# The low halves of the plain weights made by a scaling on ScalarE and an adding transfer from DRAM, with some modulation work and the feed-forward products in another order

## The chip, the cores and the metric

The kernel runs on one core of a Trainium2 chip. The time is the device time of one execution in microseconds (us), from the first instruction to the last, with what the runtime puts around it. The engines are called as in the profile: PE (TensorE, matrix products; PEld is its weight load), DVE (VectorE), ACT (ScalarE), POOL (GpSimd) and SP (SyncE, which issues most transfers). Every engine works through its own queue of instructions strictly in order.

## The reference

One inference step of one hybrid layer: an HGRN2 mixer (a gated linear recurrence, 8 heads) and a Hyena mixer (a short convolution and a long one) stand beside each other, followed by a SwiGLU feed-forward. There are 128 prompt tokens and 512 sample tokens, 640 in all, the model width is 1024, the feed-forward width 2816. Cut to what matters here:

```
mod = silu(cond) @ ada_w + ada_b          # shift, scale, gate, twice
h = x * (1 + scale1) + shift1
proj = h @ w_in                           # 1024 -> 10240 columns
q, f_fwd, f_bwd, i_raw, g_raw, hy, mg = split(proj)
o_a = hgrn2_mixer(q, f_fwd, f_bwd, i_raw, g_raw, ...)
o_b = hyena_mixer(hy, ...)
gate_a, gate_b = split(sigmoid(mg))
mix = (gate_a * (o_a @ proj_a) + gate_b * (o_b @ proj_b)) @ w_out
x = layer_norm(ALPHA * x + gate1 * mix)
h = x * (1 + scale2) + shift2
gt, up = split(h @ ffn_w_in)              # 1024 -> 2 x 2816
x = layer_norm(ALPHA * x + gate2 * ((silu(gt) * up) @ ffn_w_out))
```

Everything is float32.

## The kernel before

**Split precision.** PE multiplies in a rounded 32-bit type (fp32r in the profile). To keep float32 precision each weight and each operand is split into a high half, its rounded copy, and a low half, what the rounding left. Each product is then three passes: high by high, operand's low by high, high by weight's low. So a tile of weights needs one cast (`wh`, the high half) and one subtraction (`wl` = raw - `wh`) before its third matmul can run.

**Two kinds of weight tiles.** *Plain* weights go through one stream of 101 tiles of 128x1024 (512 KB each), in the order in which the products use them: `issue` (L346) allocates a `raw` tile (3 buffers), starts its load on SP, casts it to `wh` (on ACT at L357 for most, on DVE for some, by the string `HIE`) and subtracts to get `wl` (L181, the line of the helper for two-operand operations; on DVE, for a few early ones on POOL by `WSUB`). `wh` and `wl` have 3 buffers (slots) each, so a tile's cast waits until the unit of products three tiles earlier has let go of its slot. `advance` (L361) decides how many tiles ahead are issued. The second kind are weights of two stages that use a Strassen-like scheme with 7 products instead of 8 (class `Wino`, L626 on): `gate` loads and splits the first raw tile of a block j (`wfg` in the feed-forward), `rest` loads the second and forms sums and differences of both in place (`rf`), with splits of each (`wfa`, `wfs`, `wfu`, `wfv`). These use the same `raw` buffers.

**The stages**, by the profile's time: start, filters and tables (to about 120 us); most of `w_in` by the seven-product scheme (m1, 115 to 330); the convolution by Fourier products, 330 to 516; `proj_b` (516 to 579); the recurrence, head by head, with its own plain products (579 to 878); `proj_a` (878 to 934); `w_out` (934 to 1003); the first feed-forward product by the seven-product scheme, 22 blocks (1004 to 1282); the second, called `fo`, 22 plain units of 30 matmuls of 128x512 (1282 to 1433); the last layer norm (to 1442).

**What sets the order.** In m1 the string `PLAN` is the order: `gJ` and `wJ` are gate and rest of block J, `NJ` is product N of block J, `Qi` is half a product of the modulation with `ada_w` (`ada_quad`, L400), after which the load of the next half of `ada_w` is issued (`ada_next`, L863: `araw`, 1 MB, on POOL's queue at L397). Every second `Q` is followed by `ada_vec` (L414), which copies the product out of PSUM on ACT (`md`, L417) and transposes it on PE (`adaT`, L430) or sums it there (`adag`, L420). In the feed-forward the tuple `PERIOD` is the order inside a period j: gate and rest of the next block, then the products. Product 7 of a block is copied out by ACT (`fu`, L676) before product 4 of that block may add to the same bank (`fa`). A scheduler then places every instruction in its engine's queue, within these orders and by what it takes the durations to be.

Of the kernel before, what the change touches and what calls it, by code (L numbers as in the profile page):

```python
# [13 lines left out]
ALU = mybir.AluOpType  # L14
# [101 lines left out]
    return {k: np.ascontiguousarray(v) for k, v in c.items()}  # L116


PLAN = """x0 k0 L0 k1 x4 k2 p mlp t L1 T0 x3 T4 A0 x2 D0 T2 A1 x1 L2 B0 M0 T1 D2 A2 M2 T3 h0 L3 B1 D1 A3 h1 B2 M1 D3 h2 h3 M3 h4 W2 W0 h5 h6 h7 W1 q V0 e0 B3 g0 W3 V1 m w0 e2 10 20 g1 50 11 60 g2 70 21 30 40 w1 w2 61 51 52 12 71 Q8 62 22 g3 w3 13 41 g4 53 72 Q9 42 31 63 w4 g5 23 14 w5 73 Q10 43 32 g6 w6 64 24 15 54 74 Q11 33 65 25 44 16 26 55 75 Q12 g7 34 w7 66 45 56 17 76 Q13 35 67 46 g8 27 57 w8 18 77 Q14 g9 g10 36 w9 28 19 68 37 29 58 78 Q15 69 47 59 w10 79 Q16 38 110 210 g11 610 49 111 510 39 48 w11 211 g12 611 112 w12 212 710 Q17 g13 511 711 Q18 410 113 w13 311 612 310 411 512 712 Q19 513 213 613 412 713 312 413 313"""
HMOD = "SVSSVSSS"  # L120
HSUB = "GVVVVGVG"
WSUB = "VGGVVGGG"
# [6 lines left out]
FFNP = "1-1 2-1 g1 w1"  # L129
FFNT = ("g2", "", "")  # L130
FFN0 = "51 61 12 22 w2 71"
PERIOD = (("g", 1), ("w", 1), ("6", 0), ("4", -1), ("1", 1), ("5", 0), ("7", 0), ("3", -1), ("2", 1))
WPRI = 2
HIE = """SSSSVVSVSVSSSSSSSVVVSVVSVSSVSSSSSSSSSSSSSSSSSSSSSSSSSSSSSSSSSSSSSSSSSSSSSSSSSSSSSSSSSSSSSSSSSSSSSSSSSSSSSSSSSS"""
LOOK = """22222012202102201120122111222222222222222222222222222222222222222222222222222222222222222222222222222222222222"""
# [27 lines left out]
def body(tc, I, O):  # L163
    nc = tc.nc
    V, S, G, PE, SY = nc.vector, nc.scalar, nc.gpsimd, nc.tensor, nc.sync
# [14 lines left out]
    def tt(out, a, b, op, eng=None):  # L180
        return (eng or V).tensor_tensor(out=out, in0=a, in1=b, op=op)  # L181
# [4 lines left out]
    def f32(ap):  # L186
        return ap.bitcast(F32)

    def pool(name, bufs=1, space=None, side=None):
        kw = dict(name=name, bufs=bufs, reuse_waits="tile")  # L190
        if space is not None:
            kw["space"] = space
        if side is not None:
            kw["side"] = side
        cm = tc.tile_pool(**kw)
        p = cm.__enter__()
        return p, (lambda: cm.__exit__(None, None, None))
# [19 lines left out]
    def mm_bank(nm):  # L217
        return bank("mm", nm)
# [20 lines left out]
    w1 = sp.tile([EMB, ORD], F32, name="w1")  # L239
# [12 lines left out]
    w2 = sp.tile([P, ORD], F32, name="w2")  # L252
    w3 = sp.tile([P, 2, ORD], F32, name="w3")
# [92 lines left out]
    def issue(i):  # L346
        src, (a, b), own = stream["specs"][i]
        raw = wp.tile([P, a, b], F32, tag="raw", bufs=RAW_BUFS, name=f"raw{i}")
        SY.dma_start(raw, src)
        if own is None:  # L350
            q, th, tl, n = wp, "wh", "wl", HL_BUFS
        else:
            q, th, tl, n = own[0]["p"], "wbh", "wbl", own[1]
        hi = q.tile([P, a, b], F32R, tag=th, bufs=n, name=f"wh{i}")
        lo = q.tile([P, a, b], F32R, tag=tl, bufs=n, name=f"wl{i}")
        with tc.high_priority():
            (V.tensor_copy if HIE[i] == "V" else S.copy)(hi, raw)  # L357
            tt(lo, raw, f32(hi), ALU.subtract, G if i < len(WSUB) and WSUB[i] == "G" else V)
        stream["hl"].append((hi, lo))

    def advance(pos, n):  # L361
# [33 lines left out]
    def ada_load(nb, i, q, tag, bufs, eng=SY):  # L395
        raw = q.tile([P, 4, 512], F32, tag=tag, bufs=bufs, name=f"araw{nb}_{i}")
        eng.dma_start(raw, ada_w.rearrange("(k p) n -> p k n", p=P)[:, 4 * i:4 * i + 4, nb * 512:nb * 512 + 512])  # L397
        ada["raw"][nb, i] = raw
# [9 lines left out]
    def ada_mods(nb, q):  # L408
        with tc.high_priority():
            for i in range(2):  # L410
                ada_quad(nb, i)
            ada_vec(nb, q)

    def ada_vec(nb, q):  # L414
        part, half = nb // 2, nb % 2
        md = q.tile([P, 512], F32, tag="md", bufs=1, name=f"md{nb}")
        S.copy(md, ada["ps"].pop(nb))  # L417
        if part in (2, 5):
            p2 = mm_bank(f"adag{nb}")
            PE.matmul(p2[0:2, :], cst[:, 128:130], md, start=True, stop=True)  # L420
            gr = q.tile([2, 512], F32, tag="md", bufs=1, name=f"gr{nb}")
            SY.dma_start(gr, I["ada_b"][:, nb * 512:nb * 512 + 512].to_broadcast([2, 512]))
            tt(gr, p2[0:2, :], gr, ALU.add)
            V.tensor_scalar(gr, gr, 1.0 / ALPHA, None, ALU.mult)
            SY.dma_start(gd[part // 3, :, half * 512:half * 512 + 512], gr)
            return
        slot = {0: 0, 1: 1, 3: 2, 4: 3}[part]
        p2 = mm_bank(f"adaT{nb}")
        for i in range(4):
            PE.transpose(p2[:, i * P:i * P + P], md[:, i * P:i * P + P], ident)  # L430
        v = p2.rearrange("p (k g r) -> p k g r", k=4, g=4)[:, :, :, 0:2]
        dst = modT[:, slot, half * 4:half * 4 + 4, :]
        b0 = 17 + slot * 8 + half * 4
        tt(dst, v[:, :, 0], prT2[:, b0:b0 + 4].unsqueeze(2).to_broadcast([P, 4, 2]), ALU.add)
        for g in range(1, 4):
            tt(dst, v[:, :, g], dst, ALU.add)
# [3 lines left out]
    vp, close_vp = pool("vp")  # L440
# [7 lines left out]
    def x_load(t):  # L448
        xs = se.tile([P, D], F32, tag="xs", bufs=3, name=f"xs{t}")
        SY.dma_start(xs, x_tok[t])  # L450
        return xs

    def x_transpose(t, xs):
        for q in range(2):
            ps = sc_bank(f"xT{t}_{q}")
            for k in range(4):
                PE.transpose(ps[:, k * P:k * P + P], xs[:, (4 * q + k) * P:(4 * q + k + 1) * P], ident)
            for i in range(2):
                cpy("x", 2 * t + q, xT.tiles[2 * q + i][:, :, t * P:t * P + P],
                    ps[:, i * 256:i * 256 + 256].rearrange("p (k t) -> p k t", k=2))  # L460
# [162 lines left out]
    class Wino:  # L623
# [98 lines left out]
    def start():  # L722
        stream["stop"] = 4
        xs, ld, ab = {}, {}, {}

        def step(op, i):
            if op == "x":
                xs[i] = x_load(i)
            elif op == "T":
                x_transpose(i, xs[i])  # L730
            elif op == "L":
                ld[i] = kern_load(i)
            elif op == "A":
                ab[i] = kern_a(i, ld[i])
            elif op == "B":
                ab[i] = kern_b(i, ab[i])
            elif op == "W":
                kern_store(i, ab[i])
            elif op == "k":
                ktab(i)  # L740
            elif op == "D":
                for n in range(2):
                    ada_load(i, n, se, "araw", 3)
            elif op == "Q":
                nb, n = divmod(i, 2)
                ada_quad(nb, n)
                if i < M1_ADA[1] * 2 - 1:
                    ada_next(i + 1)
                if n == 1:
                    ada_vec(nb, mo["y"])  # L750
            elif op == "M":
                ada_mods(i, se)
            elif op == "h":
                make_h(i)
            elif op == "V":
                run_unit(vu[i])
            elif op == "e":
                m1_operands(i)
            elif op == "m":
                m1_open()  # L760
            elif op in "gw1234567":
                m1.run(op + str(i))()
            else:
                dict(p=params_load, t=params_T, q=params)[op]()

        for tok in PLAN.split():
            if tok == "mlp":
                if HP:
                    with tc.high_priority():
# [12 lines left out]
    mo = {}  # L782
# [78 lines left out]
    m1 = Wino("m", lambda tag: mo["p"], m1_x, m1_cols, m1_done, M1PRI)  # L861

    def ada_next(i):  # L863
        ada_load(*divmod(i, 2), vp, "v", 1, G)

    def m1_open():
        close_sp()
# [917 lines left out]
```

## Time and profile before

| what | number |
|---|---|
| time, median of 3 runs | 1445.78 us (1444.48 to 1446.87) |
| the profiled execution | 1444.85 us; its span is 1442.4 us |
| PE busy | 1382.4 us, 96% of the span |
| DVE, ACT, POOL busy | 998.9, 617.4, 72.6 us |
| mean granted PE clock | 0.992 of full speed |
| moved by DMA | 195.63 MB, 136 GB/s over the span |

Times in a row are microseconds from the start of the span. A row of a timeline reads: start, length, engine, line, operation, output<-inputs, shapes, count, and in brackets how long the engine had been idle and what ended that. A row of a table of groups reads: line, engine, operation, names, shapes, count, then busy us and mean ns of one, then the engine's idle time ahead of them and who ended it. A row of the DMA issues ends with the median us from issue to landing. A row of the waits says which engine and tile waited for which: us in total, times, longest.

### The profile page before, as it was taken

What the parts mean: (1) busy time and instruction counts of PE and PEld (TensorE: products, weight loads), DVE (VectorE), ACT (ScalarE), POOL (GpSimd) and SP (SyncE); (2) the same over time, 40 slices, a digit from 0 to 9 for tenths busy, and PEclk for the clock granted to TensorE, in tenths of its full rate; (3) what the DMA queues carried; (4) which work ended last, traced back from release to release, by engine and by line L of the source; (5) the groups of instructions that cost most, each with busy time, mean ns of one, the idle gap of its engine ahead of it and who ended that gap; (6) DMA issues with size and microseconds to landing.
All of it is one profiled execution on the core that took longest, in us unless ns stands there. A gap on an engine that the chain in (4) does not pass through costs nothing. (4 is left out here: it accounts for less than half of the span.)

```text
span 1442.4 us, 23457 instructions
## 1 busy us (share of the span) xinstructions
PE 1382.4 (96%) x9513; PEld 1297.4 (90%) x9513; DVE 998.9 (69%) x1751; ACT 617.4 (43%) x1011; POOL 72.6 (5%) x68
## 2 busy tenths in 40 slices
PE   5999999989999999999999999999999999999997
PEld 2698888889999998999999999988999999998886
DVE  6886775745888853638888786568977667756427
ACT  3654544432333211446665655227644344542111
POOL 4320000011000000000000000000000000000003
PEclk9999999999999999999999999999999999999999
DMA  7934665557333364432232223551343333257211
GB/s 245 327 136 139 210 194 156 169 183 251 96 92 92 107 211 146 144 119 83 63 102 61 76 57 113 180 182 73 109 123 104 108 115 106 88 177 278 83 59 73
DMA packets 195783, 195.63 MB, mean 136 GB/s; under 512 B 7581, under 2 KB 155773, under 8 KB 194908
## 3 DMA queue, kind: packets, MB, share of 16 engines
q1 hardware_dynamic: 188524, 167.17, 37.1%
q0 software_dynamic: 5424, 21.73, 4.3%
q10 hardware_dynamic: 1728, 5.24, 0.9%
q8 instruction: 74, 1.21, 0.3%
q14 instruction: 33, 0.27, 0.1%
HBM read 162.91 MB, written 31.21 MB: 135 GB/s over the span
## 5 line engine op out<-in xcount | busy, mean ns | idle before, releaser
L181 DVE TENSOR_TENSOR wl<-raw,wh 128x1024 fp32r<-128x1024 f32 x96 | 117.3, 1224 | 133.4 <-ACT wh L357 132.4
L357 ACT CAST wh<-raw 128x1024 fp32r<-128x1024 f32 x90 | 94.1, 1049 | 221.2 <-PE pb L611 41.0
L1423 PE MATMUL fo<-wh,act 128*128 128x512 f32 (+1 forms) x440 | 130.7, 380 | 0.0
L1423 PEld LDWEIGHTS fo<-wh,act 128*128 128x128 f32 x440 | 81.3, 188 | 15.9
L1423 PE MATMUL fo<-wl,act 128*128 128x512 f32 (+1 forms) x220 | 83.4, 379 | 0.0
L611 PE MATMUL hy<-hTh,wh 128*128 128x320 f32 x256 | 79.6, 311 | 0.0
L611 PE MATMUL hy<-hTh,wl 128*128 128x320 f32 x256 | 79.2, 309 | 0.0
L611 PE MATMUL hy<-hTl,wh 128*128 128x320 f32 x256 | 79.2, 309 | 0.0
L611 PE MATMUL f<-hTh,wh 128*128 128x320 f32 x224 | 70.8, 316 | 0.0
L611 PE MATMUL f<-hTl,wh 128*128 128x320 f32 x224 | 69.7, 311 | 0.0
L611 PE MATMUL f<-hTh,wl 128*128 128x320 f32 x224 | 69.3, 309 | 0.0
L181 POOL TENSOR_TENSOR y<-y,gb 128x512 f32<-128x512 f32 x8 | 11.6, 1454 | 900.8 <-ACT y L170 900.5
L1423 PEld LDWEIGHTS fo<-wl,act 128*128 128x128 f32 x220 | 41.4, 188 | 7.9
L611 PEld LDWEIGHTS hy<-hTh,wh 128*128 128x128 f32 x256 | 48.1, 188 | 0.0
L611 PEld LDWEIGHTS hy<-hTl,wh 128*128 128x128 f32 x256 | 48.1, 188 | 0.0
L611 PEld LDWEIGHTS hy<-hTh,wl 128*128 128x128 f32 x256 | 48.1, 188 | 0.0
L170 ACT ACT_TABLE_LOAD x36 | 46.2, 1283 | 1.4 <-PEq L1769 0.7
L707 PE MATMUL v<-wl,hTh 128*128 128x256 f32 x160 | 44.9, 285 | 1.6 <-DVE wl L181 1.6
L707 PE MATMUL v<-wh,hTl 128*128 128x256 f32 x160 | 45.1, 285 | 0.2 <-POOL hTl L181 0.2
L707 PE MATMUL v<-wh,hTh 128*128 128x256 f32 x160 | 44.8, 285 | 0.0
L611 PEld LDWEIGHTS f<-hTl,wh 128*128 128x128 f32 x224 | 42.2, 188 | 0.0
L611 PEld LDWEIGHTS f<-hTh,wh 128*128 128x128 f32 x224 | 42.2, 188 | 0.0
(2291 smaller groups left out, 4730.9 us busy)
## 6 DMA issues: line engine op xcount, KB each, us to landing
raw<-in_w_in SPq DMA_DIRECT2D x52, 512.0 KB, 3.8
rf<-in_ffn_w_in SPq DMA_DIRECT2D x42, 512.0 KB, 4.0
araw<-in_ada_w POOLq DMA_DIRECT2D x16, 1024.0 KB, 5.7
rm<-in_w_in SPq DMA_DIRECT2D x28, 512.0 KB, 3.8
raw<-in_ffn_w_out SPq DMA_DIRECT2D x22, 512.0 KB, 3.7
sd<-my SPq DMA_DIRECT2D x28, 320.0 KB, 3.6
araw<-in_ada_w SPq DMA_DIRECT2D x8, 1024.0 KB, 11.3
kk<-kd SPq DMA_DIRECT2D x20, 256.0 KB, 3.1
```

Of the source, the lines that this page charges most:

```text
L170: r = S.activation(out, in_, func, bias=bias, scale=scale)
L181: return (eng or V).tensor_tensor(out=out, in0=a, in1=b, op=op)
L357: (V.tensor_copy if HIE[i] == "V" else S.copy)(hi, raw)
L611: r = PE.matmul(ps[:, 0:HT], w[a][:, k, :], x[b][:, k, c0:c0 + HT], start=k == 0 and i == 0, stop=k == kt - 1 and i == 2)
L707: PE.matmul(ps[:, (t - t0) * 256:(t - t0) * 256 + 256], hT[b][:, k, t * P:t * P + P], w[a][:, k % 4, :], start=k == 0 and i == 0, stop=k = ...
L1423: PE.matmul(ps, x(t, b, k0 + kk), w[a][:, kk, :], start=first and kk == 0 and i == 0, stop=last and kk == nk - 1 and i == 2)
```

## The change

There are four edits.

1. From the ninth plain tile on (`i >= len(WSUB)`, which is 8), the low half is no longer raw - high by one subtraction. ACT writes the raw weights times -1 into `wl`, whose type rounds them, so that it holds the negated high half; then POOL's queue starts a transfer that reads the same weights from DRAM once more and adds them to what `wl` holds. 93 tiles go this way; 93 subtractions leave DVE, 93 scalings come to ACT and 93 adding transfers of 512 KB to POOL's queue.
2. The loads of `ada_w` in m1 that `ada_next` issues go from POOL's queue to SP's (12 of them).
3. `ada_vec` no longer follows the second `Q` at once: `PLAN` has tokens `Z4` to `Z9` for it, some products later.
4. `PERIOD` has product 1 of the next block ahead of product 4 of the last one.

```
-PLAN = """... 73 Q10 43 32 ... 75 Q12 g7 34 ... 77 Q14 g9 ... 110 210 g11 ... 612 310 411 ... 413 313"""
+PLAN = """... 73 Z4 Q10 43 32 ... 75 Q12 Z5 g7 34 ... 77 Z6 Q14 g9 ... 110 210 Z7 g11 ... 612 Z8 310 411 ... 413 313 Z9"""
-PERIOD = (("g", 1), ("w", 1), ("6", 0), ("4", -1), ("1", 1), ("5", 0), ("7", 0), ("3", -1), ("2", 1))
+PERIOD = (("g", 1), ("w", 1), ("6", 0), ("1", 1), ("4", -1), ("5", 0), ("7", 0), ("3", -1), ("2", 1))
@@ issue
             (V.tensor_copy if HIE[i] == "V" else S.copy)(hi, raw)
-            tt(lo, raw, f32(hi), ALU.subtract, G if i < len(WSUB) and WSUB[i] == "G" else V)
+            if i < len(WSUB):
+                tt(lo, raw, f32(hi), ALU.subtract, G if WSUB[i] == "G" else V)
+            else:
+                S.mul(lo, raw, -1.0)
+                G.dma_start(lo, src, accum_op=ALU.add)
@@ step, op "Q" and a new op "Z"
-                if n == 1:
-                    ada_vec(nb, mo["y"])
+            elif op == "Z":
+                ada_vec(i, mo["y"])
@@ ada_next
-        ada_load(*divmod(i, 2), vp, "v", 1, G)
+        ada_load(*divmod(i, 2), vp, "v", 1)
```

How the queues change at three places:

ACT's queue where the last two tiles of the recurrence's `v` products are made, at 597 to 602 us of the profile before. Each tile's cast is `wh<-raw`. Before:

```order
L170 ACTIVATE gg_6072<-bt_6152 128x10x4
L170 ACTIVATE xx_6076<-bt_6152 128x10x2
L709 COPY v_6188<-v_2_6239 128x512
L357 CAST wh_6318<-raw_6316 128x1024
L357 CAST wh_6324<-raw_6322 128x1024
L709 COPY v_6188<-v_4_6289 128x256
```

and now:

```order
L170 ACTIVATE gg_6096<-bt_6177 128x10x4
L170 ACTIVATE xx_6100<-bt_6177 128x10x2
L713 COPY v_6214<-v_2_6265 128x512
L357 CAST wh_6344<-raw_6342 128x1024
L361 ACTIVATE wl_6345<-raw_6342 128x1024
L357 CAST wh_6351<-raw_6349 128x1024
L361 ACTIVATE wl_6352<-raw_6349 128x1024
L713 COPY v_6214<-v_4_6315 128x256
```

Each cast has got the scaling right behind it. The transfers that complete the two tiles are in POOL's queue, which there holds nothing else.

ACT's queue in one period of the first feed-forward product (the split of blocks 13 and 14; `fu_11<-fa` is the copy of block 11's product 7 that product 4 of block 11 waits for, `fc_12` that of product 1 of block 12). Before:

```order
L619 CAST wfa13h<-rf_13_11973 128x512
L619 CAST wfg14h<-rf_14_12098 128x1024
L676 COPY fc_12_11904<-fa_11891 128x320
L619 CAST wfs13h<-rf_13_11967 128x512
L619 CAST wfu13h<-rf_13_11973 128x1024
L676 COPY fu_11_11931<-fa_11760 128x320
L619 CAST wfv13h<-rf_13_11967 128x512
```

and now:

```order
L680 COPY fc_12_11962<-fa_11949 128x320
L623 CAST wfg14h<-rf_14_12169 128x1024
L623 CAST wfa13h<-rf_13_12044 128x512
L680 COPY fu_11_12002<-fa_11818 128x320
L623 CAST wfu13h<-rf_13_12044 128x1024
L623 CAST wfs13h<-rf_13_12038 128x512
L623 CAST wfv13h<-rf_13_12038 128x512
```

The copy of product 7 now stands ahead of the casts `wfu13h` and `wfs13h`, and the cast of the later block's gate, `wfg14h`, ahead of `wfa13h`.

DVE's queue in the same period. Before:

```order
L181 TENSOR_TENSOR wfa13l<-rf_13_11973,wfa13h 128x512
L181 TENSOR_TENSOR rf_13_11973<-rf_13_11973 128x512
L181 TENSOR_TENSOR wfg14l<-rf_14_12098,wfg14h 128x1024
L181 TENSOR_TENSOR rf_13_11973<-rf_13_11967,rf_13_11973 128x512
L181 TENSOR_TENSOR rf_13_11967<-rf_13_11973,rf_13_11967 128x512
L181 TENSOR_TENSOR rf_13_11967<-rf_13_11967 128x512
L181 TENSOR_TENSOR wfs13l<-rf_13_11967,wfs13h 128x512
L181 TENSOR_TENSOR wfu13l<-rf_13_11973,wfu13h 128x1024
L181 TENSOR_TENSOR fu_11_11931<-fc_11906,fu_11_11931 128x320
L181 TENSOR_TENSOR wfv13l<-rf_13_11967,wfv13h 128x512
```

and now:

```order
L181 TENSOR_TENSOR wfg14l<-rf_14_12169,wfg14h 128x1024
L181 TENSOR_TENSOR wfa13l<-rf_13_12044,wfa13h 128x512
L181 TENSOR_TENSOR rf_13_12044<-rf_13_12044 128x512
L181 TENSOR_TENSOR rf_13_12044<-rf_13_12038,rf_13_12044 128x512
L181 TENSOR_TENSOR rf_13_12038<-rf_13_12044,rf_13_12038 128x512
L181 TENSOR_TENSOR fu_11_12002<-fc_11977,fu_11_12002 128x320
L181 TENSOR_TENSOR rf_13_12038<-rf_13_12038 128x512
L181 TENSOR_TENSOR wfu13l<-rf_13_12044,wfu13h 128x1024
L181 TENSOR_TENSOR wfs13l<-rf_13_12038,wfs13h 128x512
L181 TENSOR_TENSOR wfv13l<-rf_13_12038,wfv13h 128x512
```

Two operations on block 13, `wfa13l` and the first `rf_13`, stood ahead of the gate of block 14 and now stand behind it.

More of the change, by code (lines that the diff above doesn't have):

```diff
@@ L116, in _constants @@
     return {k: np.ascontiguousarray(v) for k, v in c.items()}
-PLAN = """x0 k0 L0 k1 x4 k2 p mlp t L1 T0 x3 T4 A0 x2 D0 T2 A1 x1 L2 B0 M0 T1 D2 A2 M2 T3 h0 L3 B1 D1 A3 h1 B2 M1 D3 h2 h3 M3 h4 W2 W0 h5 h6 h7 W1 q V0 e0 B3 g0 W3 V1 m w0 e2 10 20 g1 50 11 60 g2 70 21 30 40 w1 w2 61 51 52 12 71 Q8 62 22 g3 w3 13 41 g4 53 72 Q9 42 31 63 w4 g5 23 14 w5 73 Q10 43 32 g6 w6 64 24 15 54 74 Q11 33 65 25 44 16 26 55 75 Q12 g7 34 w7 66 45 56 17 76 Q13 35 67 46 g8 27 57 w8 18 77 Q14 g9 g10 36 w9 28 19 68 37 29 58 78 Q15 69 47 59 w10 79 Q16 38 110 210 g11 610 49 111 510 39 48 w11 211 g12 611 112 w12 212 710 Q17 g13 511 711 Q18 410 113 w13 311 612 310 411 512 712 Q19 513 213 613 412 713 312 413 313"""
+PLAN = """x0 k0 L0 k1 x4 k2 p mlp t L1 T0 x3 T4 A0 x2 D0 T2 A1 x1 L2 B0 M0 T1 D2 A2 M2 T3 h0 L3 B1 D1 A3 h1 B2 M1 D3 h2 h3 M3 h4 W2 W0 h5 h6 h7 W1 q V0 e0 B3 g0 W3 V1 m w0 e2 10 20 g1 50 11 60 g2 70 21 30 40 w1 w2 61 51 52 12 71 Q8 62 22 g3 w3 13 41 g4 53 72 Q9 42 31 63 w4 g5 23 14 w5 73 Z4 Q10 43 32 g6 w6 64 24 15 54 74 Q11 33 65 25 44 16 26 55 75 Q12 Z5 g7 34 w7 66 45 56 17 76 Q13 35 67 46 g8 27 57 w8 18 77 Z6 Q14 g9 g10 36 w9 28 19 68 37 29 58 78 Q15 69 47 59 w10 79 Q16 38 110 210 Z7 g11 610 49 111 510 39 48 w11 211 g12 611 112 w12 212 710 Q17 g13 511 711 Q18 410 113 w13 311 612 Z8 310 411 512 712 Q19 513 213 613 412 713 312 413 313 Z9"""
 HMOD = "SVSSVSSS"
```

## The prediction

> **What bounds the kernel now.** I read the page's busy times first, then the waits of PE, then the groups of the low-half work, and last the timelines at the places where a low half or a load comes late.
>
> ```profile
> PE 1382.4 (96%) x9513; PEld 1297.4 (90%) x9513; DVE 998.9 (69%) x1751; ACT 617.4 (43%) x1011; POOL 72.6 (5%) x68
> PE fa L668 <- ACT fu L676: 8.5, 12, 1.3
> PE adaT L430 <- ACT md L417: 3.6, 2, 1.9
> PE adag L420 <- ACT md L417: 1.0, 1, 1.0
> PE v L707 <- DVE wl L181: 1.6, 2, 1.0
> L181 DVE TENSOR_TENSOR wl<-raw,wh 128x1024 fp32r<-128x1024 f32 x96 | 117.3, 1224 | 133.4 <-ACT wh L357 132.4
> L357 ACT CAST wh<-raw 128x1024 fp32r<-128x1024 f32 x90 | 94.1, 1049 | 221.2 <-PE pb L611 41.0
> ```
>
> PE is busy 1382.4 of 1442.4 us, so all its idle time is 60 us, and no edit can give back more. Of that, the plain low halves hold PE up twice, for 1.6 us, the longer time in the start stage, which the change leaves alone. So what the 93 subtractions cost DVE (117.3/96 x 93 = 114 us) is no cost to the end: DVE itself mostly waits for the casts ahead of them (132.4 us). Edit 1 can gain next to nothing directly; it can only make low halves later. What can be gained lies in the other rows: 8.5 us in the feed-forward (`fa<-fu`, the wait that edit 4 moves) and 3.6 + 1.0 = 4.6 us in m1 (the modulation waits that edit 3 moves).
>
> **Edit 1, price of a low half.** ACT: 93 scalings of the tile that the cast takes 1.05 us for, so 98 us more on an engine busy 43%; a table load comes with none of them, the queue has 36 before and now. Then the adding transfer, which the trace doesn't have. Call D its time from issue to landing.
>
> ```profile
> raw<-in_w_in SPq DMA_DIRECT2D x52, 512.0 KB, 3.8
> rf<-in_ffn_w_in SPq DMA_DIRECT2D x42, 512.0 KB, 4.0
> araw<-in_ada_w POOLq DMA_DIRECT2D x16, 1024.0 KB, 5.7
> araw<-in_ada_w SPq DMA_DIRECT2D x8, 1024.0 KB, 11.3
> L397 POOL DMA_DIRECT2D araw<-in_ada_w x16 | 12.0, 753 | 378.4 <-PE fw L974 170.4 <-PE ada L406 167.1 <-ACT mc L676 31.2
> ```
>
> From below it is a plain load of the same 512 KB, 3.8 us. Its engine must also fetch what it adds to, so the bytes read are 1 MB: on POOL's queue 5.7 us, which I take. From above, the 1 MB loads in the crowded start, 11.3 us. Starting one holds POOL 0.75 us, and POOL has 5% of work. So a low half is ready 1.05 (cast) + 1.05 (scaling) + D = 7.8 us after its slot and raw tile are there, against 1.05 + 1.22 = 2.3 before. Its `wl` and its transfer hold nothing else: behind the transfer on POOL stand other such transfers, in order of use.
>
> The Trainium skill bears on D in two places. "DMA: Bandwidth & Descriptors", section "Anatomy of one DMA — SWDGE (gpsimd) path", fits 2.0 us plus bytes by 436 GB/s, which gives an estimate of 3.2 us for 512 KB and 4.4 us for twice that; by 4.4 the two stalls below would shrink by 1.3 us each. "Collectives: The Full Stack", section "The bandwidth ceiling: the fold count and why AG ≠ RS ≠ AR", says that an add in a DMA needs two source reads and moved about half of what a copy did (32.35 against 62.28 GB/s); that speaks against the change, and no trace here shows it yet.
>
> **Where 7.8 us is too long.** A tile's lead is the time from the last matmul of the unit that had its slot to its own first low matmul. Where units of 7 us follow each other (`proj_a`, `w_out`, `fo`, 46 units), three slots give two units, about 14 us:
>
> ```profile
> 878.19 56.33 PE pa L611 x384
> 1282.26 81.24 PE fo L1423 x360
> ```
>
> (56.33 us for 8 units is 7.04 us each, 81.24 us for 12 is 6.8.) There 7.8 fits and costs nothing; the cover goes at D = 14 - 2.1 = 11.9. In the recurrence a unit's slot is free much earlier than it is needed. Two places have short leads. The last `v` tiles:
>
> ```profile
> 599.12 1.05 ACT L357 CAST wh<-raw 128x1024 fp32r<-128x1024 f32 x1 [0.78 <-PE v L707]
> 601.68 1.22 DVE L181 TENSOR_TENSOR wl<-raw,wh 128x1024 fp32r<-128x1024 f32 x1
> 602.95 0.39 PE L707 MATMUL v<-wl,hTh 128*128 128x256 f32 x1 [0.68 <-DVE wl L181]
> ```
>
> The slot frees as the cast starts; PE already waits 0.68. Now cast and scaling end at 601.2, the low half lands at 601.2 + D, and PE waits D - 1.75 more than before: +4.0 at D = 5.7, from +2.0 (3.8) to +9.5 (11.3). The scheduler could hide this only with other products in front, and the queue has none. The last `fo` unit:
>
> ```profile
> 1405.54 1.05 ACT L357 CAST wh<-raw 128x1024 fp32r<-128x1024 f32 x1 [5.85 <-PE fo_last L1423]
> 1406.62 1.23 DVE L181 TENSOR_TENSOR wl<-raw,wh 128x1024 fp32r<-128x1024 f32 x1 [5.67 <-ACT wh L357]
> 1410.05 0.39 PE L1423 MATMUL fo<-wl,act 128*128 128x512 f32 x1
> ```
>
> Ready at 1405.54 + 2.1 + D = 1407.6 + D, wanted between 1410.05 and 1410.5 (which of the low matmuls in a row is the unit's first, I can't tell): +2.8 at 5.7, from +0.9 to +8.4. It stands near the end, so nothing after it takes it back.
>
> **More traffic.** 93 x 512 KB = 48.8 MB more is read. Averaged that is nothing, but at the start of `fo` the transfers are already full:
>
> ```profile
> 1285.00:1295.00 10.00, 10.00 (x45) 8.29 (x45) 7.02 (x9) 5.53 (x8) 0.00 (x0) 1.00 0.85 281
> 1295.00:1305.00 10.00, 10.00 (x45) 8.27 (x45) 6.38 (x8) 6.81 (x10) 0.00 (x0) 1.00 0.95 310
> 1305.00:1315.00 10.00, 10.00 (x46) 8.28 (x45) 8.79 (x10) 1.06 (x2) 0.00 (x0) 1.00 0.99 388
> 1316.51 1.05 ACT L357 CAST wh<-raw 128x1024 fp32r<-128x1024 f32 x1 [10.46 <-DMA raw<-in_ffn_w_out]
> 1319.36 2.35 DVE L181 TENSOR_TENSOR wl<-raw,wh 128x1024 fp32r<-128x1024 f32 x2
> 1323.37 0.39 PE L1423 MATMUL fo<-wl,act 128*128 128x512 f32 x1
> ```
>
> (The last three columns of a window are PE's clock, the share of the 16 DMA engines, GB/s.) A raw tile lands only at 1316.51; its low half is ready at 1320.6 and wanted about 1323.4. Now it would be 1316.51 + 2.1 + 5.7 = 1324.3, a stall of 0.9, if the raw tile came as early. But three adding transfers, for the casts of the tiles before it, fall into these full windows: 1.5 MB at 388 GB/s push it back 4 us, twice that if each byte is read twice; part of it falls into gaps. I take 3 us, so +4.0; from 0 to +9.
>
> **Edits 2 and 3, m1.** The three modulation waits (1.9, 1.6, 1.0 us) go, because several products of 1.76 us now stand between ACT's copy and PE's use of it: -4.6. The 12 loads on SP's queue follow the half product that frees their buffer, so they hold SP's own loads up little, but each puts 1 MB ahead of a raw tile of the next block. I charge 1.1: -3.5, from -4.6 to +3 (half a microsecond for six of the twelve).
>
> **Edit 4, feed-forward.** The period now, in ACT's, DVE's and SP's timelines, PE's wait, and the chain that ends last:
>
> ```profile
> 1149.66 1.05 ACT L619 CAST wfg14h<-rf 128x1024 fp32r<-128x1024 f32 x1 [2.41 <-DMA rf<-in_ffn_w_in]
> 1153.34 0.62 ACT L619 CAST wfs13h<-rf 128x512 fp32r<-128x512 f32 x1 [2.30 <-DVE rf L181]
> 1154.81 0.42 ACT L676 COPY fu<-fa 128x320 f32<-128x320 f32 x1
> 1155.28 0.42 PE L668 MATMUL fa<-t4h,wfa11h 128*128 128x320 f32 x1 [1.08 <-ACT fu L676]
> 1147.29 0.69 DVE L181 TENSOR_TENSOR wfa13l<-rf,wfa13h 128x512 fp32r<-128x512 f32 x1 [1.86 <-ACT wfa13h L619]
> 1148.01 0.69 DVE L181 TENSOR_TENSOR rf<-rf 128x512 f32<-128x512 f32 x1
> 1154.94 1.23 DVE L181 TENSOR_TENSOR wfu13l<-rf,wfu13h 128x1024 fp32r<-128x1024 f32 x1 [0.25 <-ACT wfu13h L619]
> 1156.48 0.68 DVE L181 TENSOR_TENSOR wfv13l<-rf,wfv13h 128x512 fp32r<-128x512 f32 x1
> 1156.19 1.75 SPq L633 DMA_DIRECT2D rf<-in_ffn_w_in x2
> 1103.58 5.42 DMA rf<-in_ffn_w_in
> 1221.85 6.10 DMA rf<-in_ffn_w_in
> 1239.12 1.76 PE fa L668 x12
> ```
>
> Seven products of 1.76 us are 12.3 us of PE; the loads come every (1221.85 - 1103.58)/9 = 13.1 us. So the loop of load, splits and freed raw buffers is the slower one, and PE waits about 0.8 us a period, by way of the copy at 1154.81, which ACT reaches only behind `wfs13h` and `wfu13h`. The change frees PE of that: the copy can run at 1151.2, 3.6 us sooner, and product 4 comes one product, 1.76 us, later, so PE gets 5.4 us of play. That is gained once, not in each period, while the loop stays as long as it is. And it gets longer. Now `wfa13l` and the first `rf` run at 1147.3 to 1148.7, in the gap in which DVE waits for the gate's load. In the new order both stand behind `wfg14l`, so behind the load: the splits that free the raw buffers end 0.61 + 0.70 = 1.3 us later, less about 0.2 to 0.5 because the cast of `wfu13` no longer waits for `wfs13`. I take 0.9 us a period for 11 periods that are so ordered, 9.9 - 5.4 = +4.5; from -5.4 (the loads come sooner and hide it) to +9.9 (the play is no use).
>
> **Sum.** 4.0 + 2.8 + 4.0 - 3.5 + 4.5 = +11.8. The profiled run took 1444.85 (2.45 of it outside the span); that gives 1456.7, and on the median of the runs, 0.9 higher, 1457.6. I forecast **1457**.
>
> **Rivals.** *Faster:* the released copy in the feed-forward decides. If the loop stays at 13.1 us or shortens, because the loads land at least 0.9 us sooner than those that the chain shows (5.4 to 6.1 us against a median of 4.0 for all 42 of them), the 5.4 us of play are a gain. With D at 3.8 the other terms are 2.0 + 0.9 + 0 - 3.5 = -0.6, so from a feed-forward term of -2.3 on the kernel is faster; with all of it and m1's 4.6 it is -7.1, 1439. For it: the wait that goes is PE's largest, and those loads are late only because two share the way; against it: DVE's new order, and 3.8 is the lowest that D can be. *Level:* D is 5.7 with its 4.0 + 2.8, `fo`'s start has cover, and the released copy gives 4 of its 5.4: 6.8 - 3.5 - 4 = -0.7, about 1445. *Much slower:* the adding transfer takes longer than the 11.9 us that the 7 us units cover. Then three slots turn in 7 + 2.1 + D instead of 21 us: at D = 16 each of the 46 units takes 8.4 instead of 7, +64 and the rest with it, above 1520. For it: nothing here shows how fast a DMA adds, and 1 MB once took 11.3; against: that was in the crowded start.
>
> **Chances.** Forecast 0.50, faster 0.25, level 0.14, much slower 0.11. About 0.2%, 2.9 us, is what a measurement of this kernel can tell. Of the forecast's 0.50 all but 0.01 is slower by over that; of the level case 0.10 is within it, 0.04 split on both sides: faster 0.27, same 0.11, slower 0.62. The range 1438 to 1473 leaves out much slower and some of the fastest; the forecast's own is 1449 to 1470.
>
> **What would show it.** The median of the new row of adding transfers gives D; under 4.5 or over 11.9 the sum is wrong. PE's waits should show the adding transfer ahead of `v<-wl` (4 to 5 us at 600) and in the last `fo` unit. In the feed-forward the loads should come every 14 us instead of 13.1; if `fa<-fu` is gone and they come every 12.3 to 13, edit 4 is a gain and I am wrong there. `adaT` and `adag` should wait for nothing in m1.

## The result, and the profile after

The changed kernel takes 1487.08 us (1484.65 to 1490.43, four runs) against 1445.63 us before (1444.48 to 1446.87): 1.0288 times as long, 95% interval 1.0266 to 1.0310. That is 41.5 us slower; 11.8 were forecast, and the time lies above the range. From the page after and its view of the transfers:

```profile
span 1488.7 us, 23649 instructions
PE 1396.3 (94%) x9513; PEld 1304.4 (88%) x9513; DVE 889.7 (60%) x1658; ACT 705.9 (47%) x1104; POOL 196.4 (13%) x149
q0 software_dynamic: 73792, 57.92, 25.5%
HBM read 211.67 MB, written 31.21 MB: 163 GB/s over the span
raw<-in_w_in SPq DMA_DIRECT2D x52, 512.0 KB, 4.0
wl<-in_w_in POOLq DMA_DIRECT2D x44, 512.0 KB, 7.5
wl<-in_ffn_w_out POOLq DMA_DIRECT2D x22, 512.0 KB, 7.8
wl<-in_w_out POOLq DMA_DIRECT2D x8, 512.0 KB, 10.7
```

DVE has lost its 93 subtractions (its busy time falls by 109 us) and ACT has got 93 scalings, whose own row sums to 98.1 us, as reckoned. PE's idle time has grown from 60 to 92.4 us (1488.7 - 1396.3), and its busy time by 14 us for the same 9513 matmuls: the mean granted clock of this execution is 0.982, where it was 0.992. An adding transfer of 512 KB, 5.7 us in the forecast, takes 7.5 to 10.7 us in the middle. The waits of PE that are new or larger, in the view of the waits:

```profile
PE fc L672 <- DVE fu L181: 17.6, 10, 2.1
PE fo L1427 <- DMA wl<-in_ffn_w_out: 12.5, 2, 9.5
PE v L711 <- DMA wl<-in_w_in: 9.5, 2, 5.2
PE wo L1427 <- DMA wl<-in_w_out: 3.6, 4, 2.2
PE f L615 <- DMA wl<-in_w_in: 2.5, 1, 2.5
```

Where the time went is seen best from when each stage's first product starts. The row of a tile's matmuls gives it (the times behind the durations are the first and the last start); here for the convolution's `hy` and the second feed-forward product `fo`, first before, then after:

```profile
L611 PE MATMUL hy<-hTh,wh x256: 303/309/395, 329.1 to 486.8; 128*128 128x320 f32 x128
L1423 PE MATMUL fo<-wh,act x440: 277/390/399, 1282.1 to 1430.1; 128*128 128x512 f32 x133, 128*128 128x256 f32 x14
```
```profile
L615 PE MATMUL hy<-hTh,wh x256: 303/309/394, 309.2 to 467.1; 128*128 128x320 f32 x128
L1427 PE MATMUL fo<-wh,act x440: 277/389/628, 1308.3 to 1474.3; 128*128 128x512 f32 x133, 128*128 128x256 f32 x14
```

The convolution begins 19.9 us earlier, `fo` 26.2 us later. All stages read in this way, in us (the last column is what each stage adds to the span):

| from the first product of ... to that of ... | before | after | difference |
|---|---|---|---|
| start to the convolution (m1 is in it) | 329.1 | 309.2 | -19.9 |
| convolution and `proj_b`, to the recurrence | 249.9 | 250.0 | +0.1 |
| recurrence, to `proj_a` | 299.0 | 319.6 | +20.6 |
| `proj_a`, to `w_out` | 56.4 | 56.6 | +0.2 |
| `w_out`, to the first feed-forward product | 58.4 | 69.3 | +10.9 |
| first feed-forward product, to `fo` | 289.3 | 303.6 | +14.3 |
| `fo`, to its last matmul | 151.2 | 169.2 | +18.0 |
| behind it | 9.1 | 11.2 | +2.1 |

So in these two traces the change is a gain of 20 us and a loss of 66; the difference, 46.3, is more than the 41.5 of the medians, because the profiled execution is the slowest of the four. The forecast had the sign of every stage right except for `w_out`, which it put at nothing, and nearly every size wrong.

What the loss is made of, the busy times and clocks of the stages tell (view of the windows, one window for each stage). In the recurrence, `w_out`, the first feed-forward product and `fo` PE stands idle for 14.3, 7.1, 21.2 and 12.8 us, where it was 2.1, 0, 11.3 and 0: 42 us more. And the granted clock, 1.00 in all four before, is 0.98, 0.95, 0.99 and 0.96: by the length of each stage times what is missing of the clock, an estimate, 20 us more. In `w_out` these two rows are the longest waits:

```profile
970.19 0.79 PE L1427 MATMUL wo<-wl,mixh 128*128 128x512 f32 x1 [2.21 <-DMA wl<-in_w_out]
983.93 1.11 PE L1496 MATMUL xh<-cst,r 128*128 128x128 f32 x4 [3.44 <-ACT r L170]
```

The second is not a wait for a low half: the layer norm's work on ACT stands behind two casts of the next tiles, whose raw loads end only at 973.2 and 978.5. With edit 1 alone it doesn't appear.

### The profile page after: what moved, and what is told of

The parts are those of the page before. It is cut to its first block, busy times and chain, and to the rows that moved or that the text cites. A ratio compares the mean times of both kernels' runs of the same rounds, so it can differ in the third digit from the quotient of the medians.

```text
span 1488.7 us, 23649 instructions
## 1 busy us (share of the span) xinstructions
PE 1396.3 (94%) x9513; PEld 1304.4 (88%) x9513; DVE 889.7 (60%) x1658; ACT 705.9 (47%) x1104; POOL 196.4 (13%) x149
## 3 DMA queue, kind: packets, MB, share of 16 engines
q0 software_dynamic: 73792, 57.92, 25.5%
## 4 chain that ended last, share of the span: by engine, by line
PE 50%; issue 20%; DMA 11%; DVE 11%; ACT 5%; POOL 3%; SPq 0%; DVEq 0%; POOLq 0%; ACTq 0%
PE hy L615 8%; PE f L615 6%; DMA rf<-in_ffn_w_in 5%; PE ma L672 4%; PE pa L615 4%; PE g L615 3%; PE fa L672 3%; PE mc L672 2%; POOL wl L362 2%; DVE rf L181 2%; PE fw L978 2%; PE inv L1013 2%; PE fc L672 1%; DMA rm<-in_w_in 1%; DMA raw<-in_w_out 1%
## 5 line engine op out<-in xcount | busy, mean ns | idle before, releaser
L362 POOL DMA_DIRECT2D wl<-in_w_in x44 | 67.4, 1531 | 382.9 <-ACT wl L361 278.6
L361 ACT ACTIVATE wl<-raw 128x1024 fp32r<-128x1024 f32 x93 | 98.1, 1055 | 15.5 <-PE hy L615 10.3
L1427 PE MATMUL fo<-wl,act 128*128 128x512 f32 (+1 forms) x220 | 85.3, 390 | 12.5 <-DMA wl<-in_ffn_w_out 12.5
L362 POOL DMA_DIRECT2D wl<-in_ffn_w_out x22 | 26.5, 1202 | 439.7 <-ACT wl L361 430.4
L181 DVE TENSOR_TENSOR tmb<-fo,gate 128x512 f32<-128x512 f32 (+1 forms) x11 | 6.7, 613 | 94.7 <-PE fo L1427 94.7
L1135 DVE SCALAR_TENSOR_TENSOR g<-g,prT,g 128x320 f32<-128x320 f32 x16 | 8.8, 551 | 82.2 <-ACT g L170 82.2
```

The source lines that it names most:

```text
L361: S.mul(lo, raw, -1.0)
L362: G.dma_start(lo, src, accum_op=ALU.add)
L1135: V.scalar_tensor_tensor(o[:, cs], ps[:, 0:HT], norm_w, o[:, cs], ALU.mult, ALU.mult)
L1427: PE.matmul(ps, x(t, b, k0 + kk), w[a][:, kk, :], start=first and kk == 0 and i == 0, stop=last and kk == nk - 1 and i == 2)
```

## The experiments

The theory after the comparison: edits 2 and 3 give the 20 us of m1, edit 4 lengthens the feed-forward loop, and edit 1 costs where a tile's lead is shorter than scaling and adding transfer. Times are medians; each kernel is set beside runs of the kernel before on the same chip, whose median was 1446.98 us in the first four experiments, 1444.58 in the next four, 1444.38 in the four after them and 1444.66 in the last three.

### The edits one by one

**Edits 2 and 3 alone.**

```
 PLAN and op "Z" as changed; ada_next: ada_load(..., "v", 1)   # SP's queue
 issue and PERIOD as before
```


> Only edits 2 and 3 (the loads of ada_w on SP's queue, the modulation step later in PLAN); low halves and the feed-forward order as before. In the two traces the convolution's first hy product starts at 329.1 us before and at 309.2 after, so m1 gave 20 us, not the 3.5 forecast. Theory (the gain is of edits 2 and 3 alone): 1446 - 20 = 1426 us. Rival (a part of it comes from the lighter load that edit 1 puts on DVE or from raw buffers freed sooner): 1430 to 1442.

1427.52 us, ratio 0.9863 (0.9846 to 0.9880): 19.5 us faster. The whole gain belongs to these two; the rival falls.

**Edit 4 alone.**

```
-("6", 0), ("4", -1), ("1", 1), ("5", 0), ...
+("6", 0), ("1", 1), ("4", -1), ("5", 0), ...
```


> Only edit 4 (product 1 of the next block ahead of product 4 of the last). Between the first fg product and the first fo product lie 289.3 us before and 303.6 after. Theory (the new order lengthens the loop of loads and splits by 0.9 us or more a period, with no adding transfer in that stage): 1446 + 14 = 1460 us, PE waiting for fc<-fu in 10 periods. Rival (the order alone is harmless and the loop was lengthened by transfers or by other orders of edit 1): 1440 to 1448.

1453.77 us, 1.0047 (1.0030 to 1.0063): 6.8 us slower, about half of the 14 us that the stage lost in the changed kernel. The stage takes 298.1 us here. The wait `fa<-fu` does not go by this edit alone (6.6 us in 11 periods, 8.5 in 12 before), and `fc<-fu`, 0.5 us before, takes 7.5 us in 13 periods.

**Edit 1 alone.**

```
-            tt(lo, raw, f32(hi), ALU.subtract, ...)
+            S.mul(lo, raw, -1.0)                        # from the ninth tile on
+            G.dma_start(lo, src, accum_op=ALU.add)
```


> Only edit 1 (negated high half and adding transfer). Theory: it carries the losses seen after in the recurrence (+21 us between the last pb and the first pa product), w_out (+11) and fo with the tail (+20): 1446 + 52 = 1498 us. Rival (after, the recurrence and fo lost so much because m1's gain of 20 us put their loads closer together, or because of edits 2 to 4): less than 1480.

1493.07 us, 1.0317 (1.0299 to 1.0335): 46.1 us slower, with stalls for `wl` at `v`, `f`, `w_out` and `fo` like those of the changed kernel. The rival falls.

**Edits 2, 3 and 4.**

> Edits 2, 3 and 4 without edit 1. If the edits add up: 1446 - 20 + 14 = 1440 us; if edit 4 is harmless without edit 1, 1426.

1433.48 us, 0.9910 (0.9893 to 0.9926): -19.5 + 6.0; these edits add up. **Edits 1, 2 and 3:**

> Edits 1, 2 and 3 without edit 4. If the edits add up: 1447 + 46 - 19.5 = 1474 us. The first feed-forward product took 303.6 us with all edits, 298.1 with edit 4 alone and 291.0 with edit 1 alone; if edits 1 and 4 disturb each other there, leaving edit 4 out gives 12 us, 1474, and if edit 4 costs only its own 7 us, 1480.

1477.52 us, 1.0219 (1.0185 to 1.0252). The intervals of this and the changed kernel's ratio nearly meet (1.0252, 1.0266), so how much edit 4 costs beside edit 1 is known only as about 10 us. The stage itself is clearer in the traces: 293.1 us here, 303.6 with edit 4 too, so 10.5 beside edit 1 against 7 to 9 without it.

### What m1's gain is

**Edit 3 alone, and edit 2 alone.**

```
 edit 3 alone: ada_load(..., "v", 1, G) stays; Z tokens in PLAN
 edit 2 alone: ada_load(..., "v", 1); ada_vec still behind the second Q
```


> Only edit 3 (ada_vec later in PLAN); the loads of ada_w stay on POOL's queue. Theory (the order in PLAN is what freed m1): most of the 19.5 us, 1427 to 1433. Rival (the loads on SP's queue matter): 1438 or more.

> Only edit 2 (the loads of ada_w in m1 on SP's queue). Theory (the order in PLAN is what freed m1): no gain, 1444 to 1449. Rival (it is the loads' place): 1435 or less.

Edit 3: 1442.71 us, 0.9990 (0.9973 to 1.0008), no difference. Edit 2: 1428.51, 0.9887 (0.9863 to 0.9910). My theory falls: it is the loads' place, not the later modulation step. Why, ACT's timeline shows. Before:

```profile
122.20 1.05 ACT L619 CAST wmg2h<-rm 128x1024 fp32r<-128x1024 f32 x1 [1.61 <-DMA rm<-in_w_in]
123.16 0.42 ACT L676 COPY mc<-ma 128x320 f32<-128x320 f32 x1
126.71 0.62 ACT L619 CAST wma1h<-rm 128x512 fp32r<-128x512 f32 x1 [3.14 <-DMA rm<-in_w_in]
127.24 0.42 ACT L676 COPY mu<-ma 128x320 f32<-128x320 f32 x1
127.71 0.41 PE L668 MATMUL ma<-m7h,wmu0h 128*128 128x320 f32 x1 [3.18 <-ACT mu L676]
```

With edit 2 alone:

```profile
122.22 1.05 ACT L619 CAST wmg2h<-rm 128x1024 fp32r<-128x1024 f32 x1 [1.75 <-DMA rm<-in_w_in]
123.17 0.42 ACT L676 COPY mc<-ma 128x320 f32<-128x320 f32 x1
123.71 0.43 ACT L676 COPY mu<-ma 128x320 f32<-128x320 f32 x1
126.25 0.43 ACT L676 COPY mu<-ma 128x320 f32<-128x320 f32 x1 [2.12 <-PE ma L668]
126.65 0.62 ACT L619 CAST wma1h<-rm 128x512 fp32r<-128x512 f32 x1
```

Before, the copy `mu`, for which PE waits, stands behind a cast that waits for its load until 126.71, and PE loses 3.18 us. With the 1 MB loads on the queue that also brings the weights, the scheduler, which lays out ACT's queue by when it takes the loads to be there, puts two copies ahead of that cast. The loads got no faster by it: the middle one of the 28 `rm` loads takes 6.1 us instead of 3.8. So at this place the gain is one of order in ACT's queue. That the same order with the loads on POOL's queue would give it too wasn't tried.

The longest of m1's waits, 4.00 us for `mc<-mu` at 307.01, went in another way. Before, POOL and DVE subtract at the same time, and DVE's operation, 1.22 us long with edit 2 alone, takes 3.37 and holds up the sum `mu` behind it:

```profile
302.15 2.72 POOL L181 TENSOR_TENSOR wl<-raw,wh 128x1024 fp32r<-128x1024 f32 x1 [7.50 <-DVE wh L357]
302.58 3.37 DVE L181 TENSOR_TENSOR wmu13l<-rm,wmu13h 128x1024 fp32r<-128x1024 f32 x1
```

With edit 2 alone `wmu13l` runs at 288.31, POOL's subtraction only at 292.89. All in all the waits that went make up for only a part of the 18.5 us by which the stage is shorter (329.1 against 310.6). From 90 us on, before and with edit 2 alone (behind the length of the window stand the busy times of PE, PEld, DVE, ACT and POOL, then PE's clock, the share of the 16 transfer engines and GB/s):

```profile
90.00:329.10 239.10, 224.16 (x1496) 206.50 (x1496) 158.97 (x258) 111.25 (x191) 14.14 (x14) 0.97 0.54 172
90.00:310.60 220.60, 216.90 (x1495) 200.38 (x1495) 155.29 (x258) 112.68 (x191) 5.10 (x2) 1.00 0.59 186
```

PE's idle time falls by 11.2 us (14.9 to 3.7), and its busy time by 7.3 for the same matmuls, as the clock is 1.00 instead of 0.97.

### What edit 1's loss is

**The adding transfers left out, and made plain.**

```
 all four edits, and
-                G.dma_start(lo, src, accum_op=ALU.add)
+                                                     # first kernel: nothing
+                G.dma_start(lo, src.bitcast(F32R))   # second kernel: no adding
```


> All four edits, but the adding transfers are left out: the low half stays the negated high half, so the third pass of the plain products works on other numbers; everything else, the 93 scalings on ACT too, is as in the change. Theory (the adding transfer is what loses the time): the losses of the recurrence, w_out, fo and the tail go, and the time is that without edit 1, 1433 us, within 4. Rival (the scalings in ACT's queue delay casts and copies): half or more of the 54 us between that kernel and the changed one stays, so over 1455.

> All four edits, but the transfers overwrite instead of adding: each brings the raw weights into the low half, on POOL's queue, with the same bytes read from DRAM; so the low half is the raw weight and the third pass works on other numbers. Theory (adding makes the transfer slow): the transfer takes 4 to 5 us instead of 7.5 to 10.7, the stalls shrink by 3 us or more each, and the time is 1445 to 1460. Rival (the price is the second read of 49 MB and the issue on POOL, whatever it does): 1475 or more.

Without them 1441.17 us, 0.9971 (0.9960 to 0.9982); with plain ones 1453.57, 1.0058 (1.0036 to 1.0079). So by the ratios the loss of edit 1 splits in three: scalings and the order that comes with them 0.61% (0.9971 - 0.9910), some 9 us; the second read as a plain transfer 0.87%, 13 us; that it adds, 2.30%, 33 us. The first theory held for most of it, with a rest of 9 us that it didn't have; in the traces 5.5 of these lie in the first feed-forward product (303.9 us against 298.4), where the waits `fc<-fu` sum to 16.0 us instead of 7.8, `fa<-fu` goes (5.9) and the mean clock is 0.98 instead of 0.99. The other 3.5 lie in the recurrence (302.6 against 299.1), there without any stall over 1.2 us and at a clock of 1.00. There the order of PE's queue has changed: the small products `sc` of one head, which ran in one batch, run in two with other shapes in between, and the 512 of them take 30.0 us from start to start instead of 26.5. Which reordered instruction lengthens the waits `fc<-fu` stays open. Where the adding costs, the rows of the plain kernel tell:

```profile
q0 software_dynamic: 73792, 57.92, 20.4%
wl<-in_w_in POOLq DMA_DIRECT2D x44, 512.0 KB, 5.8
wl<-in_ffn_w_out POOLq DMA_DIRECT2D x22, 512.0 KB, 5.0
wl<-in_w_out POOLq DMA_DIRECT2D x8, 512.0 KB, 7.6
```

The same packets and bytes kept the 16 DMA engines for 20.4% of 1451.8 us, 296 us, and when they add for 25.5% of 1488.7, 380 us. From issue to landing adding costs 1.7 to 3.1 us a tile.

**The tiles with long leads, and the others.**

```
+            if 8 <= i <= 30 or 38 <= i <= 67 or 90 <= i <= 96:   # first kernel, 60 tiles
+            if 31 <= i <= 37 or 68 <= i <= 89 or i >= 97:        # second kernel, 33 tiles
+                S.mul(lo, raw, -1.0)
+                G.dma_start(lo, src, accum_op=ALU.add)
             else:
                 tt(lo, raw, f32(hi), ALU.subtract, ...)
```


> Edits 2 and 3, and edit 1 for 60 of its 93 tiles: those whose slot is free some 14 us or more ahead (convolution, proj_b, the recurrence from its f and g products on, proj_a, the middle of fo). The v tiles and their two followers, w_out, the gate tiles of the feed-forward, the first 11 and the last 4 tiles of fo keep the subtraction on DVE. Theory (a tile costs time only where its lead is shorter than scaling + transfer): 1427.5, at most 4 more. Rival (each adding transfer costs something wherever it stands, by its traffic or by its place in POOL's and ACT's queues): 60/93 of 46 us, so about 1457.

> The complement: edits 2 and 3, and edit 1 for the other 33 tiles alone (the v tiles and their followers, w_out, the gate tiles, the first 11 and last 4 of fo). Theory: nearly all of edit 1's 46 us, 1465 to 1474. Rival (cost in proportion to the number of tiles): 33/93 of 46, about 1444.

60 tiles: 1429.24 us, 0.9889 (0.9853 to 0.9926), no different from edits 2 and 3 alone within the intervals. 33 tiles: 1475.13, 1.0213 (1.0175 to 1.0252), 47.6 us above them by the medians. The rival, cost by the number of tiles, falls plainly; the stalls are a matter of lead. That the 60 tiles cost nothing at all isn't shown: in the traces the recurrence takes 303.5 us with them against 299.0, with PE's `sc` products in two batches as above and no new stall, and the first feed-forward product 288.8 against 291.9, a stage that takes between 289.3 and 291.9 in kernels that don't differ in it. The rows of one of the shapes of `sc`, with edits 2 and 3 alone and with the 60 tiles:

```profile
L1244 PE MATMUL sc<-t,t 128*32 128x32 f32 x256 | 5.2, 196 | 0.0
L1248 PE MATMUL sc<-t,t 128*32 128x32 f32 x256 | 7.1, 197 | 0.0
```

**Two of those places by themselves.**

```
+            if 31 <= i <= 37:    # first kernel: the v tiles and their followers
+            if 79 <= i <= 89:    # second kernel: the first 11 tiles of fo
```


> Edits 2 and 3, and edit 1 for seven tiles alone, the v tiles of the recurrence and their followers (31 to 37). In the changed kernel PE stood still 12 us there, but that stage grew by 20 us. Theory (a stall costs its own length and then again because PE's granted clock is lower for some 40 us, 0.83 to 0.96 in the windows from 560 to 620 us): 1427.5 + 16 to 20 = 1444 to 1448, with 12 us of stalls. Rival (the rest of the 20 us comes from the other 86 tiles): 1427.5 + 12 = 1440 or less.

> Edits 2 and 3, and edit 1 for the first 11 tiles of fo alone. Theory (three adding transfers in the fullest windows push the next raw tile back and its own adding transfer then takes 9.5 us): one stall of 8 to 11 us some 42 us into fo, the slow clock behind it, 1427.5 + 11 to 15 = 1438 to 1443. Rival (the stall needs the adding transfers of the gate tiles and of the stages before): under 1433.

The seven tiles cost 16.2 us (1443.69 us, 0.9985, 0.9968 to 1.0001). PE's stalls on them add up to 4.29 + 5.08 + 2.87 = 12.2 us, so 4 us came on top. (The medians are of different chips; in the traces the recurrence takes 314.4 us instead of 299.0, 15.4 more, for 11.5 us more of idle time.) They are in PE's granted clock, the third number from the end of a window:

```profile
560.00:580.00 20.00, 15.71 (x108) 15.51 (x107) 9.32 (x22) 8.79 (x11) 2.58 (x2) 0.91 0.78 186
580.00:600.00 20.00, 14.92 (x111) 14.71 (x110) 8.85 (x11) 9.03 (x13) 2.84 (x2) 0.84 0.70 152
600.00:620.00 20.00, 17.13 (x129) 16.86 (x128) 1.23 (x1) 8.44 (x11) 3.10 (x2) 0.99 0.66 151
```

With edits 2 and 3 alone the same windows have a clock of 1.00. The Trainium skill, "TensorE: Matmul & The Clock Gate", section "Part 1: The HAM clock gate (the "warmup" mystery)", says that activity of PE is what releases its throttle, and that some 3.4 us of it are needed; the trace agrees with that: in narrow windows the clock is 0.50 behind the first stall, from 573.2 to 576.4 us, and during the end of the second and behind it, from 593.6 to 600.3. Together the stalls cost about a third more than their length. Shorter ones can do so too: in the changed kernel PE has ten stalls of 2.0 us or more from the recurrence on, and during eight of them or within 1.5 us behind, the windows show 0.50 for 3 us or more.

The 11 tiles of `fo` cost 13.3 us (1440.85 us, 0.9979, 0.9969 to 0.9988; `fo` itself takes 164.9 us instead of 151.2), with one stall of 9.82 us, so the stall is of `fo`'s own making. In the changed kernel it reads:

```profile
1325.00:1335.00 10.00, 10.00 (x46) 8.29 (x45) 4.79 (x6) 6.40 (x9) 1.63 (x2) 1.00 1.05 336
1335.00:1345.00 10.00, 10.00 (x45) 7.97 (x44) 6.22 (x7) 1.56 (x3) 0.00 (x0) 1.00 1.05 361
1348.78 1.05 ACT L357 CAST wh<-raw 128x1024 fp32r<-128x1024 f32 x1 [12.08 <-DMA raw<-in_ffn_w_out]
1351.09 1.20 POOL L362 DMA_DIRECT2D wl<-in_ffn_w_out x1 [18.15 <-ACT wl L361]
1360.61 0.79 PE L1427 MATMUL fo<-wl,act 128*128 128x512 f32 x1 [9.51 <-DMA wl<-in_ffn_w_out]
```

The raw tile is cast 40.5 us after `fo` began, against 34.4 before (1316.51 - 1282.1), 6 us later: its load starts 29.7 us into `fo` instead of 26.0, behind the loads of `y` on SP, and takes 10.7 us. In these windows the transfer engines are full (the share of 1.05 counts each packet whole where it starts). Then its adding transfer takes 9.5 us, with two more starting right behind it; in the quieter middle of `fo` they take 7.2 to 7.9. That it is these two that slow it wasn't tried by itself.

### The feed-forward loop

**The gate's low half on POOL, from block 2, and from block 8.**

```
 edits 2 and 3, and in the first feed-forward product, for the gate's split:
-        tt(l_, src, f32(h_), ALU.subtract)
+        tt(l_, src, f32(h_), ALU.subtract, G)    # second kernel: only where j > 7
```


> Edits 2 and 3 with plain low halves and the old feed-forward order, and one thing new: in the first feed-forward product the gate's low half (wfg..l, 20 tiles of 128x1024) is subtracted on POOL instead of DVE. Theory (the loop of loads and splits on DVE, 13.1 us a period against 12.3 of products, bounds that stage, and this takes 1.2 us out of it): PE's waits of 10 us there mostly go, 1418 to 1421. Rival (the loop hangs on ACT's queue or the loads, or POOL's subtraction of 2.6 us slows DVE): 1426 to 1430.

> Edits 2 and 3, plain low halves, the old feed-forward order, and the gate's low half on POOL from block 8 of the first feed-forward product on. With it from block 2 the late periods ran at 12.5 us with no stall, but PE waited 9 us in the first blocks, where POOL's 2.5 us subtraction is in the way. Theory (the loop on DVE bounds the late periods only): 1427.5 - 6 to 9 = 1418.5 to 1421.5. Rival (what is won in the late periods is lost where POOL's work slows DVE, one rf operation 2.8 us instead of 0.7): 1425 or more.

From block 2: 1426.13 us, 0.9867 (0.9839 to 0.9896), no different; PE had no stall from block 5 to block 17, but 9.9 us before that. From block 8: 1419.99 us, 0.9828 (0.9809 to 0.9846). The chain that ends last shows the loads in the late periods; here the first two and the last two of eight:

```profile
1111.57 6.04 DMA rf<-in_ffn_w_in
1122.93 4.08 DMA rf<-in_ffn_w_in
1186.88 6.05 DMA rf<-in_ffn_w_in
1199.31 5.92 DMA rf<-in_ffn_w_in
```

12.5 us a period, (1199.31 - 1111.57)/7, against 13.1 before; the stage takes 284.1 instead of 291.9 us, and in it PE waits for ACT's copy `fu` twice, 4.3 us, instead of 13 times, 10.5 us. So DVE's queue did bound the loop in the late periods. This kernel is the fastest of all: 24.7 us below the kernel before, and some 5 to 7 us below edits 2 and 3 alone (the two intervals touch; the stage's 7.8 us say it more clearly).

## Why the prediction was wrong

The step that failed is the price of edit 1. The sum had 4.0 + 2.8 + 4.0 = 10.8 us for it; by itself it costs 46.1. Three things in that price were wrong, the time D of the transfer, the list of the places with too short a lead, and what a stall costs. Edit 4 was underrated too. Against this, m1 gave 16 us more than its term, so the forecast as a whole missed by less than its price of edit 1 did: that is luck.

**Price of a low half: the size was off.** D was put at 5.7 us, from the 1 MB load on POOL's queue, because the bytes read are the same. Measured are 7.5 to 10.7, and 6.4 for the shortest of the 93, so the estimate of 4.4 is too low as well. A plain transfer of these tiles on POOL's queue already takes 5.0 to 7.6 in this traffic, so the row of `araw` was no measure even without adding, and adding comes on top. POOL needs 1.55 us to start one for `w_in`, a block of 1024 pieces of 512 bytes, where 0.75 was quoted for `araw`; of this, 0.88 stay when the transfer doesn't add.

**Which leads are too short: the list was too short.** With D = 5.7 I counted two places. With 7.5 and more there are more: the first of the last `v` tiles (4.25 us), the one I had (5.21, forecast 4.0), the follower `f` (2.50), four in `w_out` (3.6), and the end of `fo` (2.96, forecast 2.8). The mechanism and the rule were right for the stalls: the 60 tiles with some 14 us of lead brought no new one, and the 33 others brought them all. The bound of 11.9 us, from which the units of 7 us would all stall, was not reached, except in the fullest windows, where single transfers took up to 14.7. What lead doesn't tell is the 3.5 to 4.5 us of the recurrence, which come with the scalings, by way of the order of PE's queue.

**A stall costs its own length: this was wrong.** Every term of the sum took a stall at face value. The seven `v` tiles cost 16.2 us for 12.2 us of stall. This alone adds a third to the terms for `v` and `fo`. For the same reason PE's 60 us of idle time were no bound on what an edit can give back: busy time shrinks too when a stall goes, in m1 by 7.3 us.

**More traffic at the start of `fo`: right in kind, too small.** +4.0 was taken and 9 was the upper end; the stall was 9.5. The raw tile came 6 us later instead of 3, and D was 9.5 there.

**`w_out`: a term at nothing.** Its eight units were among those in which 7.8 us fit. The stage lost 10.9: 3.6 us in four waits for low halves (D was 10.7 there), 3.4 behind loads that came late, and some 3.5 by the clock of 0.95 (69.3 x 0.05, an estimate).

**Edits 2 and 3, m1: the wrong mechanism.** I counted only the waits that the moved modulation step names, 4.6 us, and charged for the loads on SP. Edit 3, which was to bring the gain, brings none that shows; edit 2, which was to cost, brings it. The waits `ma<-mu` and `mc<-mu`, 3.9 and 5.7 us in the view of the waits, I had read as belonging to the splits. Edit 2 changes the queue of ACT, an engine that it doesn't touch, by way of the scheduler, and the time at which POOL's subtraction falls, and nearly all of them went, with the slow clock behind them. The comparison of ACT's queue would have shown the first beforehand: I looked there in the feed-forward and not in m1.

**Edit 4: the loop right, the play wrong.** The loads come every 14.4 us in the changed kernel, the forecast said 14:

```profile
1204.62 5.95 DMA rf<-in_ffn_w_in
1219.04 5.93 DMA rf<-in_ffn_w_in
1233.44 5.45 DMA rf<-in_ffn_w_in
```

In the changed kernel the wait `fa<-fu` is gone as expected (with edit 4 alone 6.6 us of it stay), but the 5.4 us of play were not gained: in its place product 5 waits for DVE (`fc<-fu`, 17.6 us in 10 periods), as DVE's order now puts those sums behind the splits. The term was +4.5 with +9.9 as its end; the stage lost 14.3. Of this 7 to 9 us are edit 4's own, and some 5 appear with edit 1's scalings even without transfers.

**The rivals.** The one of a much slower kernel was right that the adding transfer was unknown and slow, but put the price at the 46 units in a row, most of which hold. The faster one was right about m1's direction only; the level one needed D at 5.7 and cover at `fo`'s start, and neither was so.

## What to carry to other kernels

Before work is moved from an idle-tolerant engine into a transfer, list each tile's lead, from its buffer's release to its first use, and compare the shortest ones with the whole new path as it is in that stage's traffic; the average hides them, and here 33 of 93 tiles carried all the stalls for low halves. An engine with a planner in front of its queue can change through an edit elsewhere, so the queues of all engines are to be compared around every wait of the bound engine, not only where the edit stands. And a stall of PE can be dearer than its length: here stalls of 2 us and more mostly had a stretch at half clock with them.

## What the runs showed of the hardware

Adding in a transfer is slow in itself, not only by the second read. From the traces' records of the single packets, mean time on one DMA engine (the plain rows of the kernel with plain transfers, the adding row of the changed kernel):

```
packets of        512 bytes   2048 bytes
SP's queue, plain     29 ns       100 ns
POOL's queue, plain   56 ns       105 ns
POOL's queue, adding  66 ns       192 ns
```

So adding takes nearly twice as long for packets of 2 KB (192 against 105). For 512 bytes a plain packet of POOL's queue takes twice as long as one of SP's (56 against 29; in the median 42 against 27); whether the queue does it or the traffic beside it, no run here separates. For the 2 KB packets that agrees with what the Trainium skill, "Collectives: The Full Stack", section "The bandwidth ceiling: the fold count and why AG ≠ RS ≠ AR", says of an add's two source reads, though its figures are those of a collective.

POOL and DVE also get in each other's way: while POOL subtracts one gate tile, an operation of DVE on a tile in SBUF takes 2.8 us instead of 0.7 (in the kernel with the gate's low half on POOL from block 8, where POOL subtracts from 1130.38 to 1132.95; the case in m1 above is another):

```profile
1130.72 2.78 DVE L181 TENSOR_TENSOR rf<-rf 128x512 f32<-128x512 f32 x1
1133.42 0.68 DVE L181 TENSOR_TENSOR wfs13l<-rf,wfs13h 128x512 fp32r<-128x512 f32 x1
```

So of the 1.2 us taken off DVE more came back in the same period. The gain, as I read the two timelines, is that the load no longer stands ahead of the other block's splits in DVE's queue: with edits 2 and 3 alone DVE idles 1.6 us for the cast of `wfg14h`, and the sums of block 13 come only behind it.
